# The modulation's matrix-vector product moved to TensorE, and another order of the first loads

## The chip, the cores and the metric

The kernel runs on one core of one Trainium2 chip. The metric is the device time of one execution in microseconds (us), the lower the better. Five engines run side by side, each with its own queue of instructions in program order: TensorE (PE in the profile, with its weight loads as PEld), VectorE (DVE), ScalarE (ACT), GpSimd (POOL), and SyncE, which here only issues the loads from memory (its queue is SPq in the profile).

## The reference, cut to what matters

Two transformer blocks run over 256 tokens (272 in the second block) of width 1024. The change touches the modulation of the first block only: one row vector, `silu(c)`, times a 1024 x 6144 matrix, whose 24 MB have to come from memory.

```python
def first_block(x, c, ada_w, ada_b, ln1_g, ln2_g, w_in, ...):
    cond = jax.nn.silu(c)                                   # [1, 1024]
    mod = (cond @ ada_w[l] + ada_b[l])[:, None, :]          # [1, 1, 6144]
    sh1, sc1, g1, sh2, sc2, g2 = jnp.split(mod, 6, axis=-1)
    h = rms_norm(x, ln1_g[l]) * (1.0 + sc1) + sh1
    x = x + g1 * hybrid_mixer(h, w_in[l], w_out[l], ...)    # two kinds of attention
    h = rms_norm(x, ln2_g[l]) * (1.0 + sc2) + sh2
    x = x + g2 * sparse_moe(h, router_w[l], ..., exp_w1[l], exp_w2[l], ...)   # 32 experts, top 4
    return x
# second_block(x, ...): attention, MLP, a linear recurrence, MLP
```

All is float32. `sc1` and `sh1` are needed ahead of the first product, `g1` by the products with `w_out`, `sc2` and `sh2` by the routing, `g2` behind the experts.

## The kernel before, in words

The kernel works in transposed form: a matrix of 256 tokens lies as eight tiles of [128 channels x 256 tokens]. In time it has three stretches: the first block up to the routing (0 to 262.9 us in the trace), the 32 experts (262.9 to about 1222 us), and the second block.

**Loads.** A list of 1 MB loads is written out by hand (`queue_pre`, L359) and issued in this order on SyncE by `Stream.pump` (L158), as soon as one of its buffers is free (`wraw` are four buffers, `wraw_r` three more at the start). One tile of the modulation's matrix is [128 x 2 x 1024]: two blocks of 128 rows, all 1024 columns of one of the six vectors. Four tiles q = 0 to 3 make a vector. In the names, s = 1 is `sc1`, 0 is `sh1`, 2 is `g1`, 4 is `sc2`, 3 is `sh2`, 5 is `g2`.

**Products.** A dense product takes a float32 weight apart into a high and a low part: ScalarE casts (L190), and GpSimd or VectorE subtracts (L192), as a string of letters, `st.cut`, says unit by unit. TensorE then runs three products per pair of tiles (L290 to L292). Its queue is in program order: a product that waits holds back all that is behind it.

**The modulation.** `ada(s, ...)` (L415) returns a list of steps. Eight steps `part(k)` each multiply a [128 x 1024] block with the column k of `cond` and add it to an accumulator, on VectorE (L435, L437), a few on ScalarE and GpSimd (L429, L431). Two steps `total(i)` transpose 4 x 128 columns each on TensorE (L449), sum them on VectorE (L452) and add them to the bias (L454). For s = 1 and 0 the steps run at the start, ahead of the first dense product; the last two blocks of s = 0 are taken in halves (L592). The steps of s = 2, 4, 3, 5 stand in the list `side`; `aux()` takes one between two dense products, if its load has been issued by then, and `side_to(n)` empties the list down to n steps. In the same way `fill()` takes one step of the attention from the list `bg`.

**Around it.** `mixer` runs the products with `w_in` (`dense_t`), interleaved with attention steps; `w_out_half(0)` and `w_out_half(4)` run the products with `w_out` and add them to the residual with `g1` (L949); between and behind them come the router's logits (L1032) and the routing (`route`), and then the experts' first products (L1440).

Of the kernel before, what the change touches and what calls it, by code (L numbers as in the profile page):

```python
# [8 lines left out]
F32 = mybir.dt.float32  # L9
# [4 lines left out]
AF = mybir.ActivationFunctionType  # L14
ALU = mybir.AluOpType
AX = mybir.AxisListType
# [4 lines left out]
S = 256  # L21
# [201 lines left out]
def add_cols(st, w, c0, ncol):  # L223

    for c in range(c0, c0 + ncol, 256):
        for k in range(0, w.shape[0], 1024):
            st.add([(_v("p (k n) -> p k n", k=8), w[k:k + 1024, c:c + 256].rearrange("(k p) n -> p k n", p=128))],
                   [lambda t, m=m: t.rearrange("p (k n) -> p k n", k=8)[:, :, m * 128:m * 128 + 128] for m in range(2)])
# [15 lines left out]
class Ker:  # L244
# [116 lines left out]
    def queue_pre(self):  # L361
# [3 lines left out]
        def add_ada(s, q):  # L365
            st.add([(_v("p (k n) -> p k n", k=2),
                     ada[q * 256:q * 256 + 256, s * 1024:s * 1024 + 1024].rearrange("(k p) n -> p k n", p=128))], ["raw"])
# [8 lines left out]
        for s in (1, 0):  # L376
            for q in range(4):
                add_ada(s, q)
        add_cols(st, w, 512, 256)
        cw = A["nsa_cmp_w1"][0]  # L380
# [34 lines left out]
    def ada(self, s, acc, pool, tag, first=0):  # L415

        nc = self.nc
        accs = [acc]

        def part(k):  # L420
            def go():
                if k % 2 == 0:
                    self.ada_t = self.st.get_raw()
                t, used = self.ada_t
                w = t[:, (k % 2) * 1024:(k % 2) * 1024 + 1024]
                if k in (1, 3, 5) and self.mid is not None:

                    b, t = self.mid[:, 0], self.mid[:, 1]
                    nc.scalar.activation(out=t if len(accs) > 1 else b, in_=w, func=AF.Copy, scale=self.cond[:, k:k + 1])  # L429
                    if len(accs) > 1:  # L430
                        nc.gpsimd.tensor_tensor(out=b, in0=b, in1=t, op=ALU.add)  # L431
                    else:
                        accs.append(b)
                elif k == first:
                    nc.vector.tensor_scalar(out=acc, in0=w, scalar1=self.cond[:, k:k + 1], scalar2=None, op0=ALU.mult)  # L435
                else:
                    nc.vector.scalar_tensor_tensor(out=acc, in0=w, scalar=self.cond[:, k:k + 1], in1=acc,  # L437
                                                   op0=ALU.mult, op1=ALU.add)
                if k % 2:
                    used()  # L440
            return go

        def total(i):
            def go():
                ps = pool.tile([128, 512], F32, name="adat", tag=tag)
                if len(accs) > 1:
                    nc.vector.tensor_tensor(out=acc, in0=acc, in1=accs.pop(), op=ALU.add)
                for m in range(4):
                    nc.tensor.transpose(ps[:, m * 128:m * 128 + 128], acc[:, i * 512 + m * 128:i * 512 + m * 128 + 128],  # L449
                                        self.c("ident"))  # L450
                t = self.pp.tile([128, 4], F32, name="adas", tag="adas", bufs=2)
                nc.vector.tensor_reduce(out=t, in_=ps.rearrange("p (m n) -> p m n", m=4), axis=AX.X, op=ALU.add)  # L452
                m4 = self.mod[:, 8 * s + 4 * i:8 * s + 4 * i + 4]
                nc.vector.tensor_tensor(out=m4, in0=t, in1=m4, op=ALU.add)  # L454
            return go

        return [part(k) for k in range(8)] + [total(i) for i in range(2)]
# [42 lines left out]
    def pre(self):  # L500
        nc, A, tc = self.nc, self.A, self.tc
        h = self.h
        X = slice(META, NT)
        ident = self.c("ident")
        with ExitStack() as ctx:
# [39 lines left out]
            self.mid = None  # L545
            acc2 = self.ar("s4", [128, 2, 1024], F32, "acc")
            acc = [acc2[:, i] for i in range(2)]
            s1, s0 = self.ada(1, acc[0], self.ps_d, "dps"), self.ada(0, acc[1], self.ps_d, "dps", 2)
            mid = [self.ar("s6", [128, 1024], F32, "mid"), vvt[:, 0:1024]]

            def by_scalar(k):

                def go():
                    if k == 0:
                        self.ada_t = self.st.get_raw()
                    t, used = self.ada_t
                    nc.scalar.activation(out=mid[k], in_=t[:, k * 1024:k * 1024 + 1024], func=AF.Copy, scale=self.cond[:, k:k + 1])
                    if k:
                        used()
                        nc.gpsimd.tensor_tensor(out=mid[0], in0=mid[0], in1=mid[1], op=ALU.add)  # L560
                return go

            s0 = [by_scalar(0), by_scalar(1)] + s0[2:]
            for f in s1[0:4]:
                f()
            rs = pp.tile([128, 3, S], F32, name="rs1", tag="hr")
            self.rsqrt(rs[:, 0], self.ss[:, :S], rs[:, 1], rs[:, 2], nc.gpsimd)
            xT = self.ar("s1", [128, 8, S], F32, "xs1")
            for k in range(8):
                nc.gpsimd.tensor_tensor(out=xT[:, k], in0=h[:, k, X], in1=rs[:, 0], op=ALU.mult)  # L570
            for f in s1[4:]:
                f()
            a1 = pp.tile([128, 8], F32, name="a1")
            nc.vector.scalar_tensor_tensor(out=a1, in0=self.mod[:, 8:16], scalar=1.0, in1=self.V8("ln1_g"),
                                           op0=ALU.add, op1=ALU.mult)
            for f in s0[0:2]:
                f()
            for k in range(8):
                nc.scalar.activation(out=xT[:, k], in_=xT[:, k], func=AF.Copy, scale=a1[:, k:k + 1])
            for f in s0[2:4]:  # L580
                f()
            nc.vector.tensor_tensor(out=acc[1], in0=acc[1], in1=mid[0], op=ALU.add)
            for f in s0[4:6]:
                f()
            nc.sync.dma_start(out=once, in_=A["once"])
            self.st.split_to(1)
            t, used = self.st.get_raw()
            for i in range(2):
                for k in (6, 7):
                    a = acc[1][:, i * 512:i * 512 + 512]  # L590
                    o = (k - 6) * 1024 + i * 512
                    nc.vector.scalar_tensor_tensor(out=a, in0=t[:, o:o + 512], scalar=self.cond[:, k:k + 1], in1=a,  # L592
                                                   op0=ALU.mult, op1=ALU.add)
            used()
            for f in s0[8:]:
                f()
# [8 lines left out]
            for s, a in ((2, 0), (4, 1), (3, 0), (5, 1)):  # L605
                self.side += [(k in (0, 2, 4, 6), f) for k, f in enumerate(self.ada(s, acc[a], self.ps_m, "m"))]

            self.side.insert(-2, (False, lambda: None))
# [10 lines left out]
    def mixer(self, H, L):  # L619
# [310 lines left out]
        self.mid = self.ar("s3", [128, 2, 1024], F32, "mid2")  # L930
        self.side_to(28)
# [23 lines left out]
        self.side_to(21)  # L955
# [4 lines left out]
        self.b1 = self.ar("b1", [64, 2048], F32R, "b1")  # L960
        self.route_early()
# [53 lines left out]
    def route_tile(self, m):  # L1015
# [35 lines left out]
        if m == 5:  # L1051
            self.side_to(11)
            self.route_bias()

    def route(self):
# [19 lines left out]

        self.h2h = self.ar("s3", [128, 2, 1024], F32R, "h2h")
# [87 lines left out]
        self.side_to(0)  # L1164
# [1075 lines left out]
```

## Time and profile before

| | us |
|---|---|
| median of 3 runs | 1898.0 (1895.3, 1898.0, 1903.77) |
| the profiled execution: its own time | 1897.58 |
| its span, from the first to the last instruction | 1895.5 |
| granted TensorE clock, mean share of full speed | 0.977 |
| PE busy | 1775.4 (94%) |
| DVE busy | 996.3 (53%) |
| ACT, POOL busy | 631.9 (33%), 403.4 (21%) |
| moved from memory | 549.60 MB, mean 290 GB/s |

The span and the time of the profiled execution differ by 2.1 us, which lie ahead of the first and behind the last instruction. The busy share is a mean over stretches that are limited by different things, so the table of stretches among the rows below is read first. In the timelines each row gives the start, the duration, the engine, the line of the kernel, the operation with its tile, and in square brackets how long the engine was idle before it and what ended that idle time. A float32 product leaves two records in the trace, one with the reduced type (fp32r) leaves one.

### The profile page before, as it was taken

Reading aid. Unit: us, or ns where it says so; the run is one execution under the profiler, and the core shown is the slowest. Engines: PE = TensorE matmul, PEld = TensorE weight load, DVE = VectorE, ACT = ScalarE, POOL = GpSimd, SP = SyncE. Lnnn points to the kernel's source line nnn. Section 1 sums busy time; section 2 is a strip of 40 time slices with the busy share of each in tenths; the row PEclk is TensorE's granted clock in tenths of the full one; section 3 lists DMA queues with packets and bytes.
Section 4 is the critical chain, followed back from the end, with each engine's and each line's share of the span. In section 5 each row is a group of like instructions: output and inputs, shape, how many; then the busy total and the mean of one; then the engine's idle time right before and its main releaser. Section 6 shows DMA issues by size and latency. Waiting matters only on the chain. (4 is left out here: it accounts for less than half of the span.)

```text
span 1895.5 us, 25891 instructions
## 1 busy us (share of the span) xinstructions
PE 1775.4 (94%) x10035; PEld 1107.9 (58%) x10035; DVE 996.3 (53%) x1620; ACT 631.9 (33%) x1110; POOL 403.4 (21%) x266
## 2 busy tenths in 40 slices
PE   3988779999999999999999999799999999889998
PEld 2866643333334343333434343387789999789986
DVE  7686744544444434444443444554575544986622
ACT  3444322111211101121110112255565544755633
POOL 4533310000000000000000000155333334554443
PEclk6999989999999999999999999899999999999999
DMA  9544789999999999999999999642245545345552
GB/s 340 207 150 134 252 326 376 423 425 424 423 425 423 425 424 406 424 423 425 423 426 423 400 424 423 225 163 74 65 134 178 179 165 169 112 133 174 182 187 80
DMA packets 183342, 549.60 MB, mean 290 GB/s; under 512 B 8656, under 2 KB 101968, under 8 KB 150256
## 3 DMA queue, kind: packets, MB, share of 16 engines
q1 hardware_dynamic: 182592, 545.99, 74.6%
q8 instruction: 80, 1.31, 0.3%
q0 software_dynamic: 432, 1.57, 0.3%
q14 instruction: 46, 0.38, 0.1%
q10 hardware_dynamic: 192, 0.35, 0.1%
HBM read 546.83 MB, written 1.05 MB: 289 GB/s over the span
## 5 line engine op out<-in xcount | busy, mean ns | idle before, releaser
L192 POOL TENSOR_TENSOR wsp<-wraw,wsp 128x1024 fp32r<-128x1024 f32 x134 | 329.6, 2463 | 1393.3 <-ACT wsp L190 1356.5
L290 PE MATMUL dps<-hn_hi,wsp 128*128 128x272 f32 (+1 forms) x832 | 248.1, 298 | 9.1 <-DVE h L1908 4.1
L190 ACT CAST wsp<-wraw 128x1024 fp32r<-128x1024 f32 x208 | 215.3, 1042 | 113.8 <-PE dps L292 51.1
L291 PE MATMUL dps<-hn_lo,wsp 128*128 128x272 f32 (+1 forms) x832 | 242.8, 292 | 1.9 <-DVE hn_lo L1636 1.9
L292 PE MATMUL dps<-hn_hi,wsp 128*128 128x272 f32 (+1 forms) x832 | 242.3, 291 | 0.0
L1571 DVE SCALAR_TENSOR_TENSOR h<-cb,vec,h 128x256 f32<-128x256 f32 x256 | 111.8, 479 | 225.4 <-PE cb L1567 225.4
L1440 PE MATMUL u<-wraw_s,xs 128*64 128x512 f32 x728 | 207.6, 602 | 0.9 <-DVE gl L1470 0.9
L1468 ACT COPY gl<-u 64x512 f32<-64x512 f32 x120 | 66.7, 582 | 417.9 <-PE u L1440 356.8
L1440 PE MATMUL u<-wraw,xs 128*64 128x512 f32 x648 | 195.2, 604 | 0.0
L290 PEld LDWEIGHTS dps<-hn_hi,wsp 128*128 128x128 f32 x832 | 161.0, 194 | 14.3 <-issue 5.8
L1440 PE MATMUL u<-wraw_r,xs 128*64 128x512 f32 x544 | 164.5, 608 | 0.0
L291 PEld LDWEIGHTS dps<-hn_lo,wsp 128*128 128x128 f32 x832 | 160.6, 193 | 3.9 <-DVE hn_lo L1636 3.0
L292 PEld LDWEIGHTS dps<-hn_hi,wsp 128*128 128x128 f32 x832 | 160.8, 193 | 0.0
L1470 DVE TENSOR_TENSOR gl<-u,gl 64x512 f32<-64x512 f32 x120 | 79.1, 680 | 140.8 <-ACT gl L1468 140.8
L192 DVE TENSOR_TENSOR wsp<-wraw,wsp 128x1024 fp32r<-128x1024 f32 x74 | 96.3, 1304 | 94.1 <-ACT wsp L190 93.9
L1440 PEld LDWEIGHTS u<-wraw_s,xs 128*64 128x64 f32 x728 | 54.7, 136 | 73.9 <-issue 65.6
L2004 DVE TENSOR_TENSOR y<-r 128x272 f32<-128x272 f32 (+1 forms) x64 | 52.9, 827 | 64.6 <-ACT r L2001 64.5
L1566 PE MATMUL cb<-st,y 128*128 128x256 f32 x256 | 80.1, 336 | 6.2 <-DVE h L1571 6.2
L1440 PEld LDWEIGHTS u<-wraw,xs 128*64 128x64 f32 x648 | 49.5, 136 | 61.4 <-issue 52.4
L1542 PE MATMUL y<-wraw_s,at 128*64 128x512 f32 x368 | 82.8, 594 | 0.0
L1566 PEld LDWEIGHTS cb<-st,y 128*128 128x128 f32 x256 | 48.4, 189 | 57.4 <-issue 41.3
L1542 PE MATMUL y<-wraw_r,at 128*64 128x512 f32 x336 | 77.3, 601 | 3.7 <-SPq L1246 3.7
(508 smaller groups left out, 3275.5 us busy)
## 6 DMA issues: line engine op xcount, KB each, us to landing
wraw_s<-in_exp_w SPq DMA_DIRECT2D x147, 1024.0 KB, 14.1
wraw_r<-in_exp_w SPq DMA_DIRECT2D x120, 1024.0 KB, 15.0
wraw<-in_exp_w SPq DMA_DIRECT2D x117, 1024.0 KB, 13.5
wraw<-in_mlp_w_up SPq DMA_DIRECT2D x32, 1024.0 KB, 5.4
wraw<-in_mlp_w_down SPq DMA_DIRECT2D x32, 1024.0 KB, 4.8
wraw<-in_ada_w SPq DMA_DIRECT2D x18, 1024.0 KB, 6.3
wraw<-in_sb_w_qkv SPq DMA_DIRECT2D x12, 1024.0 KB, 5.1
wraw<-in_lru_w_in SPq DMA_DIRECT2D x8, 1024.0 KB, 5.0
```

The costliest lines, as they stand in the source:

```text
L190: nc.scalar.copy(out=hv, in_=src)
L192: e.tensor_tensor(out=lv, in0=src, in1=lr, op=ALU.subtract)
L290: mm(o, lhsT=wh, rhs=xh, start=first, stop=False)
L291: mm(o, lhsT=wh, rhs=xl, start=False, stop=False)
L292: mm(o, lhsT=wl, rhs=xh, start=False, stop=last)
L1440: mm(u[n][64 * j:64 * j + 64], lhsT=xs[:, k, o:o + 64], rhs=w[:, ns], start=(q == 0), stop=(q == 3))
L1468: nc.scalar.copy(out=o, in_=u[n][64:128])
L1470: nc.vector.tensor_tensor(out=o, in0=u[n][R], in1=o, op=ALU.add)
L1542: mm(y[n][64 * j:64 * j + 64], lhsT=at[:, k, 0:64], rhs=w[:, ws], start=(q == 0), stop=(q == 3))
L1566: mm(o, lhsT=yh[:, m * 128:m * 128 + 128], rhs=st, start=True, stop=False)
L1571: nc.vector.scalar_tensor_tensor(out=h[:, m, META:NT], in0=o, scalar=self.mod[:, 40 + m:41 + m], in1=h[:, m, META:NT], op0=ALU.mult, op1=A ...
L2004: nc.vector.tensor_tensor(out=y[:, :n], in0=r[:, :n], in1=r[:, :n], op=ALU.mult)
```

## The change

`ada(s)` now has five steps. A step `part(q)` takes one whole tile: eight float32 products on TensorE (L436), two row blocks times four quarters of 256 columns. The weight is a column of `cond` broadcast to [128 x 32], so that quarter j is written to the partitions 32j to 32j+31 of one PSUM bank. Every one of the 32 partitions of a quarter holds the same sums. For s = 1 and 0 the four tiles add up in the bank (`whole`), and one VectorE copy (L442) brings [128 x 256] to SBUF; for the other vectors each tile is copied. The one step `total` selects one partition of each quarter by small products (L452), which also add up the four copies, and VectorE adds the bias (L455). The parts of s = 2, 4, 3, 5 use the PSUM bank "tp", which one in two of the attention's transposes also uses.

In the order of the loads the first tile of `w_in` moves from behind s = 0 to between s = 1 and s = 0, and the small table `once` moves ahead. The normalization's last steps and the products of x with it (before L570) go from GpSimd to VectorE, and the first two units of `w_in` are split ahead of the parts of s = 0, their low parts on VectorE. `side` has 20 entries where it had 41, and `side_to` gets other numbers.

```diff
--- before.py
+++ after.py
@@ -373,10 +373,11 @@
                 add_ada(*rest.pop(0))
 
         w = A["w_in"][0]
-        for s in (1, 0):
-            for q in range(4):
-                add_ada(s, q)
+        for q in range(4):
+            add_ada(1, q)
         add_cols(st, w, 512, 256)
+        for q in range(4):
+            add_ada(0, q)
...
-    def ada(self, s, acc, pool, tag, first=0):
+    def ada(self, s, whole=None):
+
 
         nc = self.nc
...
+        st, parts = {}, []
+
+        def bank(name):
+            pool, tag = whole or self.ada_bank
+            return pool.tile([128, 512], F32, name=name, tag=tag)
+
+        def part(q):
             def go():
...
+                t, used = self.st.get_raw()
+                if q == 0 or not whole:
+                    st["ps"] = bank("adap")
+                ps = st["ps"][:, 0:256]
+                for i in range(2):
+                    c = self.cond[:, 2 * q + i:2 * q + i + 1].to_broadcast([128, 32])
+                    for j in range(4):
+                        o = i * 1024 + j * 256
+                        nc.tensor.matmul(ps[32 * j:32 * j + 32], lhsT=c, rhs=t[:, o:o + 256],
+                                         start=(i == 0 and (q == 0 or not whole)), stop=(i == 1 and (q == 3 or not whole)))
+                used()
+                if whole and q < 3:
+                    return
+                x = self.acc[:, s % 2, q]
+                nc.vector.tensor_copy(out=x, in_=ps)
+                parts.append(x)
             return go
 
...
+        def total():
+            ps = bank("adat")
+
+            sel = self.c("ident").rearrange("p (j a) -> p j a", j=4)[:, :, 0]
+            for b in range(2):
+                for i, x in enumerate(parts):
+                    nc.tensor.matmul(ps[:, 4 * b:4 * b + 4], lhsT=x[:, b * 128:b * 128 + 128], rhs=sel, start=(i == 0),
+                                     stop=(i == len(parts) - 1))
+            m8 = self.mod[:, 8 * s:8 * s + 8].rearrange("p (j b) -> p b j", b=2)
+            nc.vector.tensor_tensor(out=m8, in0=ps[:, 0:8].rearrange("p (b j) -> p b j", b=2), in1=m8, op=ALU.add)
+
+        return [part(q) for q in range(4)] + [total]
 
...
+            self.acc = self.ar("s4", [128, 2, 4, 256], F32, "acc")
+            s1, s0 = self.ada(1, (pa, "tp")), self.ada(0, (self.ps_m, "ot"))
             rs = pp.tile([128, 3, S], F32, name="rs1", tag="hr")
-            self.rsqrt(rs[:, 0], self.ss[:, :S], rs[:, 1], rs[:, 2], nc.gpsimd)
+            self.rsqrt(rs[:, 0], self.ss[:, :S], rs[:, 1], rs[:, 2])
...
-                nc.gpsimd.tensor_tensor(out=xT[:, k], in0=h[:, k, X], in1=rs[:, 0], op=ALU.mult)
-            for f in s1[4:]:
+                nc.vector.tensor_tensor(out=xT[:, k], in0=h[:, k, X], in1=rs[:, 0], op=ALU.mult)
+            for f in s1:
                 f()
+            nc.sync.dma_start(out=once, in_=A["once"])
             a1 = pp.tile([128, 8], F32, name="a1")
             nc.vector.scalar_tensor_tensor(out=a1, in0=self.mod[:, 8:16], scalar=1.0, in1=self.V8("ln1_g"),
                                            op0=ALU.add, op1=ALU.mult)
...
             for k in range(8):
                 nc.scalar.activation(out=xT[:, k], in_=xT[:, k], func=AF.Copy, scale=a1[:, k:k + 1])
...
+            self.st.cut = "D"
+            self.st.split_to(2)
+            self.st.cut = "PPD"
+            for f in s0:
                 f()
...
             self.side = []
-            for s, a in ((2, 0), (4, 1), (3, 0), (5, 1)):
-                self.side += [(k in (0, 2, 4, 6), f) for k, f in enumerate(self.ada(s, acc[a], self.ps_m, "m"))]
-
-            self.side.insert(-2, (False, lambda: None))
+            self.ada_bank = pa, "tp"
+            for s in (2, 4, 3, 5):
+                self.side += [(k < 4, f) for k, f in enumerate(self.ada(s))]
...
-        self.side_to(28)
+        self.side_to(15)
...
-        self.side_to(21)
+        self.side_to(10)
 
...
+        self.ada_bank = self.ps_m, "m"
...
-            self.side_to(11)
+            self.side_to(5)
...
+        self.side_to(0)
...
-        self.side_to(0)
         self.st.limit = None
 
     def gates(self, pool):
```

The loads at the start, as SyncE issues them. Before, from the tile behind the first three of s = 1 on; `ada_w` is the modulation, `in_w_in` with 128x8x256 is the first dense weight:

```order
L170 DMA wraw<-in_ada_w 128x2x1024 x4
L170 DMA wraw_r_149<-in_ada_w 128x2x1024
L170 DMA wraw_r_153<-in_w_in 128x8x256
L170 DMA wraw_r_174<-in_w_in 128x8x128 x2
L170 DMA wraw<-in_nsa_cmp_w 64x16x128 x2
L170 DMA wraw<-in_w_in 128x8x128 x2
L170 DMA wraw<-in_nsa_cmp_w 64x16x128 x2
L170 DMA wraw<-in_w_in 128x8x128 x2
L585 DMA once<-in_once 128x1465
L170 DMA wraw_r_233<-in_ada_w 128x2x1024
```

And now, from the same place on:

```order
L170 DMA wraw<-in_ada_w 128x2x1024
L170 DMA wraw<-in_w_in 128x8x256
L170 DMA wraw<-in_ada_w 128x2x1024 x2
L170 DMA wraw_r_172<-in_ada_w 128x2x1024
L170 DMA wraw_r_182<-in_ada_w 128x2x1024
L170 DMA wraw_r_192<-in_w_in 128x8x128 x2
L170 DMA wraw<-in_nsa_cmp_w 64x16x128 x2
L554 DMA once<-in_once 128x1465
L170 DMA wraw<-in_w_in 128x8x128 x2
L170 DMA wraw<-in_nsa_cmp_w 64x16x128 x2
L170 DMA wraw<-in_w_in 128x8x128 x2
L170 DMA wraw_r_262<-in_ada_w 128x2x1024
```

The dense weight went ahead of the four tiles of s = 0, and `once` ahead of the second set of the compression's weights.

TensorE at the start, before: the sum of squares (L315), the two vectors' transposes, and the first dense products (`dps`):

```order
L315 MATMUL ss<-sq,cst 128x256 x8
L449 MATMUL adat<-cst,acc 128x128 x16
L290 MATMUL dps<-hh,wsp 128x256
L291 MATMUL dps<-hl,wsp 128x256
L292 MATMUL dps<-hh,wsp 128x256
```

And now, with eight parts in the place of sixteen transposes:

```order
L315 MATMUL ss<-sq,cst 128x256 x8
L436 MATMUL adap<-wraw_r_95,cond 32x256 x8
L436 MATMUL adap<-wraw_r_97,cond 32x256 x8
L436 MATMUL adap<-wraw_r_99,cond 32x256 x8
L436 MATMUL adap<-wraw,cond 32x256 x8
L452 MATMUL adat<-cst,acc 128x4 x2
L436 MATMUL adap<-wraw,cond 32x256 x16
L436 MATMUL adap<-wraw_r_172,cond 32x256 x8
L436 MATMUL adap<-wraw_r_182,cond 32x256 x8
L452 MATMUL adat<-cst,acc 128x4 x2
L290 MATMUL dps<-hh,wsp 128x256
```

In front of the first dense product TensorE now has 64 products L436, which wait for loads, where it had waited for VectorE's sums.

VectorE in `w_out_half(0)`, before, from the last attention steps on; the rows L949 add a finished product to the residual, the rows `acc` belong to s = 3:

```order
L437 SCALAR_TENSOR_TENSOR acc<-wraw,cond,acc 128x1024
L949 SCALAR_TENSOR_TENSOR h<-dps,vec,h 128x256
L286 TENSOR_TENSOR ol<-ot,oh 128x256
L437 SCALAR_TENSOR_TENSOR acc<-wraw,cond,acc 128x1024
L949 SCALAR_TENSOR_TENSOR h<-dps,vec,h 128x256
L447 TENSOR_TENSOR acc<-acc,mid_1658 128x1024
L452 TENSOR_REDUCE adas<-adat 128x4
L454 TENSOR_TENSOR vec<-adas,vec 128x4
L949 SCALAR_TENSOR_TENSOR h<-dps,vec,h 128x256
L452 TENSOR_REDUCE adas<-adat 128x4
L454 TENSOR_TENSOR vec<-adas,vec 128x4
```

And now the same place, with two copies of s = 5:

```order
L442 COPY acc<-adap 128x256
L915 SCALAR_TENSOR_TENSOR h<-dps,vec,h 128x256
L286 TENSOR_TENSOR ol<-ot,oh 128x256
L835 COPY ap<-tp 128x384
L915 SCALAR_TENSOR_TENSOR h<-dps,vec,h 128x256
L286 TENSOR_TENSOR ol<-ot,oh 128x256
L915 SCALAR_TENSOR_TENSOR h<-dps,vec,h 128x256 x2
L442 COPY acc<-adap 128x256
L915 SCALAR_TENSOR_TENSOR h<-dps,vec,h 128x256
L455 TENSOR_TENSOR vec<-adat,vec 128x2x4
L915 SCALAR_TENSOR_TENSOR h<-dps,vec,h 128x256
```

Two multiply-adds, a sum over `mid`, the reductions and the bias sums of s = 3 are gone from between the residual adds; two copies of [128 x 256] and one bias sum stand there.

## Rows read from the trace of the kernel before

**Rows 1.** The table of stretches: us, busy us of each engine (records), clock, DMA

```profile
14.40:30.40 16.00, 1.97 (x8) 1.57 (x8) 14.55 (x13) 6.38 (x12) 14.15 (x13) 0.56 1.04 410
...
100.00:158.60 58.60, 51.52 (x371) 37.33 (x369) 47.42 (x109) 28.88 (x98) 18.46 (x8) 1.00 0.45 141
158.60:190.00 31.40, 26.87 (x174) 19.52 (x172) 19.33 (x37) 10.68 (x30) 14.38 (x13) 1.00 0.40 105
...
210.00:224.00 14.00, 7.52 (x50) 7.20 (x50) 11.19 (x14) 4.38 (x4) 8.24 (x5) 0.88 0.95 323
224.00:250.00 26.00, 20.07 (x151) 18.65 (x150) 19.74 (x25) 4.10 (x9) 6.91 (x2) 0.93 0.93 368
250.00:262.90 12.90, 5.64 (x30) 4.30 (x28) 8.08 (x34) 6.65 (x17) 3.55 (x6) 0.57 0.78 326
...
300.00:1222.00 922.00, 911.03 (x4143) 357.83 (x4139) 408.93 (x706) 154.63 (x215) 0.00 (x0) 1.00 1.00 414
```

**Rows 2.** Waits of TensorE, 263 to 1222 us: total us, times, longest us

```profile
PE u L1442 <- DMA wraw<-in_exp_w: 0.9, 1, 0.9
```

**Rows 3.** Timeline of the start, to the first dense product

```profile
30.44 1.05 ACT L190 CAST wsp<-wraw_r 128x1024 fp32r<-128x1024 f32 x1 [0.57 <-DMA wraw_r<-in_w_in]
...
38.62 1.09 PE L449 MATMUL adat<-cst,acc 128*128 128x128 f32 x4 [14.84 <-DVE acc L592]
...
41.38 0.58 PE L290 MATMUL dps<-hh,wsp 128*128 128x256 f32 x1 [0.22 <-ACT hh L601]
```

**Rows 4.** Timeline of TensorE, first dense products: the last slow and first fast ones

```profile
46.75 0.41 PE L292 MATMUL dps<-hh,wsp 128*128 128x256 f32 x1
46.97 0.34 PE L290 MATMUL dps<-hh,wsp 128*128 128x256 f32 x1
...
47.38 0.28 PE L290 MATMUL dps<-hh,wsp 128*128 128x256 f32 x1
47.50 0.28 PE L291 MATMUL dps<-hl,wsp 128*128 128x256 f32 x1
```

**Rows 5.** DMA issues of 45.9 to 46.5 us: count, KB, us to landing

```profile
wraw_r<-in_ada_w SPq DMA_DIRECT2D x1, 1024.0 KB, 7.2
```

**Rows 6.** Timeline of TensorE: a product of 32 columns (L727) among others

```profile
61.09 0.94 PE L660 MATMUL hid<-once,wraw 128*128 128x31 f32 x7
...
62.19 0.28 PE L292 MATMUL dps<-hh,wsp 128*128 128x256 f32 x1
62.40 0.62 PE L727 MATMUL hs<-sq,once 128*32 128x256 f32 x2
62.95 0.39 PE L290 MATMUL dps<-hh,wsp 128*128 128x256 f32 x1
```

**Rows 7.** Timeline of TensorE in the experts: tiles of 64 columns

```profile
613.54 0.59 PE L1440 MATMUL u<-wraw_s,xs 128*64 128x512 f32 x1
613.55 0.59 PE L1440 MATMUL u<-wraw_r,xs 128*64 128x512 f32 x1
613.98 0.59 PE L1440 MATMUL u<-wraw_s,xs 128*64 128x512 f32 x1
```

**Rows 8.** Timeline of TensorE: the four transposes of a total

```profile
99.42 0.60 PE L449 MATMUL adat<-cst,acc 128*128 128x128 f32 x4
```

**Rows 9.** Waits of TensorE, 100 to 190 us

```profile
PE sc L830 <- ACT ap L848: 4.7, 4, 1.8
```

**Rows 10.** Waits of TensorE, 190 to 250 us

```profile
PE adat L449 <- DVE acc L447: 4.8, 1, 4.8
PE lt L1032 <- DVE h L949: 4.7, 4, 2.6
```

**Rows 11.** Timeline of VectorE and GpSimd behind the last total

```profile
238.08 4.53 POOL L1046 TENSOR_TENSOR b<-b1a,b 32x2048 fp32r<-32x2048 f32 x1 [11.70 <-ACT b L1045]
238.14 4.49 DVE L454 TENSOR_TENSOR vec<-adas,vec 128x4 f32<-128x4 f32 x1
```

**Rows 12.** VectorE by line, 41.4 to 250 us: busy us, mean ns, idle before

```profile
L437 DVE SCALAR_TENSOR_TENSOR acc<-wraw,cond,acc 128x1024 f32<-128x1024 f32 x20 | 31.0, 1548 | 0.0
```

More of the change, by code (lines that the diff above doesn't have):

```diff
@@ L413, in queue_pre @@
         more(len(rest))
-    def ada(self, s, acc, pool, tag, first=0):
+    def ada(self, s, whole=None):
         nc = self.nc
-        accs = [acc]
-        def part(k):
-            def go():
[L422 to L440, printed above, removed]
-            return go
[L443 to L457, printed above, removed]
@@ L544, in pre @@
                 self.square_in(k, h[:, k, X], S)
[L545 to L565, printed above, removed]
+            self.acc = self.ar("s4", [128, 2, 4, 256], F32, "acc")
+            s1, s0 = self.ada(1, (pa, "tp")), self.ada(0, (self.ps_m, "ot"))
             rs = pp.tile([128, 3, S], F32, name="rs1", tag="hr")
-            self.rsqrt(rs[:, 0], self.ss[:, :S], rs[:, 1], rs[:, 2], nc.gpsimd)
+            self.rsqrt(rs[:, 0], self.ss[:, :S], rs[:, 1], rs[:, 2])
             xT = self.ar("s1", [128, 8, S], F32, "xs1")
             for k in range(8):
-                nc.gpsimd.tensor_tensor(out=xT[:, k], in0=h[:, k, X], in1=rs[:, 0], op=ALU.mult)
-            for f in s1[4:]:
+                nc.vector.tensor_tensor(out=xT[:, k], in0=h[:, k, X], in1=rs[:, 0], op=ALU.mult)
+            for f in s1:
                 f()
+            nc.sync.dma_start(out=once, in_=A["once"])
             a1 = pp.tile([128, 8], F32, name="a1")
@@ L575, in pre @@
                                            op0=ALU.add, op1=ALU.mult)
-            for f in s0[0:2]:
-                f()
             for k in range(8):
                 nc.scalar.activation(out=xT[:, k], in_=xT[:, k], func=AF.Copy, scale=a1[:, k:k + 1])
[L580 to L595, printed above, removed]
+            self.st.cut = "D"
+            self.st.split_to(2)
+            self.st.cut = "PPD"
+            for f in s0:
                 f()
@@ L929, in mixer @@
             self.fill()
-        self.mid = self.ar("s3", [128, 2, 1024], F32, "mid2")
-        self.side_to(28)
+        self.side_to(15)
         g1 = self.mod[:, 16:24]
```

## The prediction

> **What bounds the kernel now.** I read the table of stretches first, because the busy share over the whole span (PE 94%) hides three different programs. In the experts, 300 to 1222 us, TensorE is busy for 911.0 of 922 us [rows 1], and among its waits there only 0.9 us stand behind a load [rows 2]. So the experts last as long as TensorE needs, and when the routing ends x us earlier the kernel ends x us earlier. The memory is full there too (414 GB/s, share 1.00), but its loads wait for TensorE to free buffers. The second block is untouched. What the change is worth is therefore the shift of the routing's end, at 262.9 us, and nothing else.
>
> In front of that the reader is to see a queue that is full with holes. At the start TensorE does 1.97 us of work in 16 [rows 1]: it waits for VectorE's multiply-adds, and its first transposes come at 38.62 us, with 14.84 us idle ahead of them; the first dense product starts at 41.38 [rows 3]. In 100 to 158.6 us TensorE is idle for 7.1 us, in 158.6 to 190 for 4.5, in 210 to 224 for 6.5, in 224 to 250 for 5.9, in 250 to 262.9 for 7.3 (stretch less busy time) [rows 1]. VectorE is 81% busy in the first of these (47.42 of 58.6), and 31.0 us of VectorE's work between 41.4 and 250 us are 20 multiply-adds of the modulation, 1.55 us each [rows 12].
>
> **The start.** The load of the first dense weight is the ninth megabyte before, and ScalarE, idle for it, begins its cast at 30.44 [rows 3]; so nine megabytes are in by 30.4 us. Now the ninth is the last tile of `sh1`. The memory gives 410 GB/s in this stretch [rows 1], a megabyte in 2.5 us, so the eight parts come at the pace of the loads, and seven are done when the last lands. TensorE's queue holds them behind the sum of squares, so two buffers come free some 3 us later than before; the loads ahead fill the queue until then, so I count nothing. Behind the last landing: one part (1.2 us at full clock, 2.3 at half; 1.8 taken), and then copy, selection, bias, and the first half of x. Before, the same tail from the first transposes to the first product took 41.38 - 38.62 = 2.8 us [rows 3], with longer pieces; I take 2.3. First product at 34.5, that is **-6.9** (-8.3 to -4.4: 33.1 with everything fast, 37 if buffers or the copy's queue delay it). The dense weight, its split and the moved work on VectorE lie beside this: they land ten microseconds before they are needed.
>
> The clock: TensorE's granted share is 0.56 in 14.4 to 30.4 us [rows 1], with almost nothing on it, and the first products step by 0.22 us until 46.97 and by 0.12 at 47.38, the lower (1.2 GHz) and the upper (2.4 GHz) level [rows 4]. From 41.38 to 46.97 that is 26 products and some 2.5 us lost. With parts on TensorE every 2.5 us it may be at full speed from the start; in 250 to 262.9 us, with 5.6 us of work spread over 12.9, the share was 0.57 all the same [rows 1], so it need not be. I take half, **-1.2** (-2.5 to 0).
>
> The first tile of `g1` is issued in 45.9 to 46.5 us and needs 7.2 [rows 5]: there at 53.1 to 53.7. Its part stands some 1.5 us ahead of the products L660 at 61.09 [rows 6], an estimate from the order of the queue; 8.1 us earlier that is 51.5. TensorE waits in order where VectorE waited before: **+1.7** (0 to +4.4).
>
> **Sixteen parts among the dense products.** Each has 8 float32 products of 256 columns on 32 columns of the array, 16 records. The row of that shape is L727: from 62.40 to 62.95 for its two records; 0.12 of these 0.55 us, and 0.09 ahead of it (0.21 for a step of 0.12 [rows 4]), and 0.11 behind (0.39 against 0.28), are the change of shape, 0.32 in all, which leaves 0.21 a record [rows 6]. Whether four quarters run beside each other no row shows. Two halves do: L1440's products of two tiles start at 613.54 and 613.55, the next at 613.98, 0.43 us for a pair with 512 columns [rows 7], 0.21 for 256. So a part costs 4 x 0.213 + 0.32 = 1.17 us with four at a time, 2.0 with two, 3.7 one by one. I take the first, since the halves overlap without loss: 16 x 1.17 = **+18.7**. All of it is on the path as far as TensorE is full.
>
> The Trainium skill ("TensorE: Matmul & The Clock Gate", Measured speedup vs the span model) has three column tiles of 32 at 2.38 times one, which is 0.79 of ideal each. By that, an estimate, a part is 3.41/(4 x 0.79) + 0.32 = 1.40 us and the forecast 3.7 us later, 1899. The pairs in [rows 7] show no such loss; no run here shows four.
>
> The four totals: 16 records with 128-column weights, at 0.11 each (7 from 61.09 to 61.87, within 0.94 [rows 6]), 1.8 us, in place of two times some 0.45 (the transposes of [rows 8], of which 0.36 is their own time to the next row and 0.08 the next row's). 4 x 0.9 = **+3.6** (0 to +5).
>
> **What VectorE gives back.** 31.0 us and the sums go from it; 16 copies of [128 x 256] come, shorter than a multiply-add. In 100 to 190 us, 11.6 us of TensorE's idle time, of which 4.7 are the score products that wait for ScalarE's exponentials [rows 9]. I take two thirds, **-8** (-11.6 to 0: nothing, if that chain is bound by its own length or if the copies delay it as the sums did). In 210 to 224 us the idle is 6.5, of which 4.8 is one wait of the transposes for VectorE's sum over `mid` [rows 10], which is gone: **-5.5** (-6.5 to -4.8 plus what a copy there costs). In 224 to 250 it is 5.9, of which 4.7 are the logits waiting for the residual [rows 10]; the sums ahead of it go, but 4.5 us are a bias sum that ran beside GpSimd's [32 x 2048] sum, both as long as each other [rows 11]. What VectorE then does beside that sum will be slow instead, so **-4** (-5 to -0.5). All parts end by then, which shortens the routing's cold stretch by perhaps **-1**.
>
> **The sum.** -6.9 - 1.2 + 1.7 + 18.7 + 3.6 - 8 - 5.5 - 4 - 1 = -2.6. The profiled execution took 1897.6 us, so 1895.0; the median of the runs is 0.4 above it. Within 0.5% (9.5 us) a measurement of this kernel can't tell a change.
>
> **Rivals.** (A) *VectorE's relief is nearly whole, and parts fall into holes.* For it: 24 us of idle time between 100 and 250, nearly all behind VectorE or ScalarE. Against: several of these waits are the attention's own chain. With all 11.6, 6.5 and 5.9 gone (-6.5 more), the full clock (-1.3) and the fast start (-1.4) it is 1886, with a few parts in the routing's holes 1885: faster.
>
> (B) *Only two quarters run at a time*, as all rows show. A part is 2.0 us: 16 x 0.85 = 13.6 more, 0.8 more at the start, 1909: slower. It decides from 1.9 us a part.
>
> (C) *They run one by one*, so that the change doesn't do what it says. Then 16 x 2.56 = 41 more; at the start eight parts of 3.7 from 14.4 us end at 44, the first product at 46.5 (+12), while the wait for `g1` goes (-1.7): 1946.
>
> (D) *The bank.* Each of the 16 parts waits for its bank, and the attention's transposes behind it wait for the copy in VectorE's queue. The nearest row is the score products' longest wait, 1.8 us [rows 9]. At 0.9 us a part it is 14 us, 1909, and from there slower; at 1.8, 1924. Against it: VectorE has 25 us less to do.
>
> **Chances.** The forecast 0.57 (its own range 1886 to 1904), A 0.24, B 0.08, D 0.07, C 0.04. Of the forecast's cases about 0.03 are under 1888.5 and none above 1907.5, so faster by over 0.5%: 0.27, within: 0.54, slower: 0.19 (B, C, D). The range 1882 to 1910 leaves out C, half of D and a little of A.
>
> **What would show it.** In the changed profile: the first dense product at 33 to 37 us, and the clock in the 20 us ahead of it; the records of four L436 starting within 0.05 us of each other and a part of 1.0 to 1.4 us among dense products (B: 1.9 to 2.1; C: 3.4 or more); waits of TensorE for the copy L442 under 4 us in sum (D: over 14); the waits for L447 and L949 gone or under 2 us; and the experts as long as before within 2 us. I am wrong if the routing ends where the start's gain alone puts it, or if the experts don't follow the routing's end.

## The result and the profile after

The changed kernel took 1916.1 us (median of 6) against 1897.3 us before (6 runs): 1.009 times as long, 95% interval 1.0066 to 1.0115. One of the six runs took 2927.0 us at a mean granted clock of 0.554 and is left out of the ratio. The kernel is slower, and outside the range that was given. The profiled execution of the changed kernel, the fastest of the six, took 1911.3 us, 13.7 us more than that of before, its span 1909.5 us.

The start and the parts came out as predicted. The rows that answer to [rows 3] and [rows 6], from the timeline of TensorE (start and duration in us, engine, line, operation, tile, records, idle time before):

```profile
31.31 1.94 PE L436 MATMUL adap<-wraw_r,cond 128*32 128x256 f32 x16 [0.57 <-DMA wraw_r<-in_ada_w]
33.80 1.01 PE L452 MATMUL adat<-cst,acc 128*128 128x4 f32 x4 [0.55 <-DVE acc L442]
35.67 0.58 PE L290 MATMUL dps<-hh,wsp 128*128 128x256 f32 x1 [0.86 <-ACT hh L569]
...
71.28 0.28 PE L292 MATMUL dps<-hh,wsp 128*128 128x256 f32 x1
71.49 1.07 PE L436 MATMUL adap<-wraw_r,cond 128*32 128x256 f32 x16
72.49 0.39 PE L290 MATMUL dps<-hh,wsp 128*128 128x256 f32 x1
```

The first dense product starts at 35.67 us, 5.7 earlier. A part among dense products holds 1.00 us until the next product starts: 16 records of 0.213 us one by one would be 3.4, so the four quarters do run beside each other (in the trace the four records of a row block's quarters start within 0.02 us, and the next four 0.22 us later).

What went wrong is in the table of stretches. The columns are the stretch and its length in us, the busy us (records) of PE, PEld, DVE, ACT and POOL, the granted clock, the share of the DMA engines, and GB/s:

```profile
36.00:42.00 6.00, 6.00 (x28) 5.81 (x28) 5.69 (x13) 4.55 (x10) 1.37 (x1) 0.50 1.11 297
42.00:49.00 7.00, 3.65 (x30) 3.44 (x30) 1.14 (x1) 3.39 (x6) 3.43 (x2) 0.99 1.16 254
49.00:66.00 17.00, 17.00 (x90) 15.67 (x88) 3.63 (x12) 5.18 (x12) 4.80 (x5) 0.50 0.98 346
66.00:80.00 14.00, 14.00 (x121) 11.03 (x120) 4.06 (x13) 4.66 (x11) 2.26 (x3) 1.00 0.57 174
182.00:209.50 27.50, 27.50 (x95) 19.43 (x95) 4.95 (x12) 3.91 (x11) 4.70 (x2) 0.50 0.12 39
```

In two stretches, 17.0 and 27.5 us long, TensorE is busy all the time and its clock is at the lower of its two levels (1.2 GHz, 0.50). Two more, at 90 and 124 us, last 3.5 us each. Before, the clock was at 1.00 from 47 to 190 us:

```profile
47.00:190.00 143.00, 130.22 (x920) 101.40 (x919) 101.89 (x203) 63.59 (x178) 58.76 (x33) 1.00 0.51 164
```

At the upper level the work of these four stretches would have taken about half as long. That is an estimate of 25.8 us lost, half of 17.0 + 27.5 + 7.0.

To see where the time goes I set the 240 groups of dense products (three products each, counted in order of time) against each other. The table gives by how many us the group of a number starts later than in the profiled execution of before (its lag; negative: earlier). Later sections use the other columns.

```
group   before   changed  mixer only  start only  sum+hold   hold40
          us     kernel   (e4)        (e2)        (f2)       (h1)
   0     41.4     -5.7      0.2        -5.4        -5.7      -5.8
  16     50.6     -2.5      0.2        -3.0        -2.8      -1.8
  24     57.0      2.3      0.2         2.5        -2.7      -1.9
  32     64.2      6.4      1.3         8.5        -1.6      -0.7
  64     83.1     14.2      7.6        10.9         3.4       4.3
 112    123.9     20.5     13.0        10.8         8.2       9.0
 144    158.8     16.6      9.0        10.8         4.2       5.0
 176    190.1     28.4     20.8        10.7         2.5       3.4
 200    218.9     22.2     14.7        10.8        -3.7      -2.8
 239    248.0     19.9     12.7        11.4        -7.0      -7.9
```

The changed kernel loses at 0.5 of the clock between groups 16 and 32 (8.9 us; f2, at 1.00 there, loses 1.2), and between 144 and 176 (11.8 us; f2 gains 1.7). The experts' first product comes at 282.6 us, 19.7 later than the 262.9 of before.

Each long stretch stands behind a wait of TensorE. The rows of the first, of TensorE and ScalarE:

```profile
44.40 0.28 PE L292 MATMUL dps<-hh,wsp 128*128 128x256 f32 x1
48.03 0.38 PE L290 MATMUL dps<-hh,wsp 128*128 128x256 f32 x1 [3.35 <-ACT vvt L612]
...
45.55 1.04 ACT L190 CAST wsp<-wraw 128x1024 fp32r<-128x1024 f32 x1 [5.00 <-DMA wraw<-in_w_in]
46.50 1.47 ACT L612 COPY vvt<-dps 64x240 f32<-64x240 f32 x4
```

TensorE is now ahead of the memory. ScalarE, in program order, stands at the cast of a weight that lands at 45.5 us; the copies that empty TensorE's bank are queued behind it. The second, of TensorE, VectorE and GpSimd (`hb` are products that use 32 rows of the array):

```profile
178.18 0.28 PE L494 MATMUL dps<-wsp,hh 128*128 128x256 f32 x1
180.66 0.69 PE L708 MATMUL hb<-hr,spread 32*128 32x256 f32 x2 [2.20 <-DVE ap L835]
...
177.67 2.46 DVE L305 TENSOR_TENSOR hr<-hr 32x256 f32<-32x256 f32 x1
180.06 0.54 DVE L835 COPY ap<-tp 128x384 f32<-128x384 f32 x1
...
177.44 2.41 POOL L192 TENSOR_TENSOR wsp<-wraw,wsp 128x1024 fp32r<-128x1024 f32 x1 [1.54 <-ACT wsp L190]
```

A product of VectorE on [32 x 256] takes 2.46 us and ends within 0.3 us of GpSimd's subtraction beside it; the same operation two lines above (L303) took 0.41. It is the kind of stretch that [rows 11] show. In the kernel before no subtraction ran beside L305, and it took 0.48 us. That the subtraction is the cause was not tried by itself.

Not all of the 19.7 us reach the end. The span is only 14.0 us longer, because the experts, from their first product to their last combining product, take 962.1 us for 966.1. Near their end TensorE waits at the branch for tokens over the limit, L1246 before and L1213 now (total us, times, longest us):

```profile
PE y L1542 <- SPq L1246: 3.7, 1, 3.7
...
PE y L1509 <- PEq L1213: 1.2, 1, 1.2
...
PE cb L1533 <- DVEq L1213: 0.5, 1, 0.5
```

Behind the longer wait the clock of the kernel before is at 0.50 from 1207.6 to 1211.0 us. From the start of the experts' last product `u` of the first layer to the end of their last combining product `cb` it is 35.6 to 35.7 us in all four profiles with the four vectors on VectorE (before, e2, f4, g1) and 32.0 to 32.6 in all ten with them on TensorE. Why the branch waits less there was not tried.

### The profile page after: what moved, and what is told of

It reads as the page before. It is cut to its first block, busy times and chain, and to the rows that moved or that the text cites. A ratio compares the mean times of both kernels' runs of the same rounds, so it can differ in the third digit from the quotient of the medians.

```text
span 1909.5 us, 26638 instructions
## 1 busy us (share of the span) xinstructions
PE 1817.4 (95%) x10443; PEld 1133.3 (59%) x10443; DVE 921.9 (48%) x1588; ACT 624.0 (33%) x1103; POOL 365.9 (19%) x248
## 5 line engine op out<-in xcount | busy, mean ns | idle before, releaser
L192 POOL TENSOR_TENSOR wsp<-wraw,wsp 128x1024 fp32r<-128x1024 f32 x134 | 322.9, 2412 | 1429.3 <-ACT wsp L190 1396.1
L1407 PE MATMUL u<-wraw_s,xs 128*64 128x512 f32 x728 | 207.5, 602 | 0.9 <-DVE gl L1437 0.9
L1407 PE MATMUL u<-wraw_r,xs 128*64 128x512 f32 x648 | 195.2, 604 | 0.0
L1407 PE MATMUL u<-wraw,xs 128*64 128x512 f32 x544 | 164.2, 607 | 0.0
L1407 PEld LDWEIGHTS u<-wraw_r,xs 128*64 128x64 f32 x648 | 49.5, 136 | 61.5 <-issue 52.7
L1411 PEld LDWEIGHTS u<-b,P 64*64 64x64 f32 (+1 forms) x128 | 16.8, 132 | 103.5 <-issue 103.5
## 6 DMA issues: line engine op xcount, KB each, us to landing
wraw<-in_exp_w SPq DMA_DIRECT2D x120, 1024.0 KB, 14.9
wraw_r<-in_exp_w SPq DMA_DIRECT2D x117, 1024.0 KB, 13.7
```

Of the source, the lines that this page charges most:

```text
L192: e.tensor_tensor(out=lv, in0=src, in1=lr, op=ALU.subtract)
L1407: mm(u[n][64 * j:64 * j + 64], lhsT=xs[:, k, o:o + 64], rhs=w[:, ns], start=(q == 0), stop=(q == 3))
```

## The experiments

Two theories. **K**: the work is worth about what was forecast, and the clock makes the loss: two waits let it fall, and it stays low though TensorE is busy. **W**: the 16 parts and four totals are simply more than VectorE's relief gives back. Kernels that ran together share the runs of the kernel before; their medians (1897.5 to 1898.6) are left out below, and a ratio is to them.

**e1: more work, whose results nobody reads.** 34 products fill the two waits:

```diff
+        self.n_dt = getattr(self, "n_dt", 0) + 1
+        if self.n_dt == 2:
+            for _ in range(16):
+                self.nc.tensor.matmul(ps[:, 256:512], lhsT=wh[:, 7], rhs=xh(7), start=True, stop=True)
...
+                if group == 1 and i == 0:
+                    d = pa.tile([128, 512], F32, name="dmy", tag="tp")
+                    for _ in range(18):
+                        nc.tensor.matmul(d[:, 0:256], lhsT=H(0)[:, 0:128], rhs=H(0), start=True, stop=True)
```

> The changed kernel with 34 more products of 256 columns on TensorE whose results nobody reads: 16 behind the second dense tile, where it waits 3.35 us at 44.4 us, and 18 ahead of the first hb product at 178.5 us, where it waits 2.20 us. Theory K (the clock: the two waits let TensorE's clock fall, and 17 and 27 us of dense work then run at half speed, which costs 8.5 and 13.6 us): with less idle time the stretches at 0.5 are gone or much shorter, and the time is 1894 to 1905 us. Theory W (the added 16 parts and totals are simply more work than VectorE's relief gives back): the dummies cost 0 to 4 us more, 1916 to 1920 us.

Measured: 1904.1 us, ratio 1.0047 (1.0020 to 1.0074), 12 us less than the changed kernel, with more work. Its ten runs spread from 1898.5 to 1917.5 us, and the profile is of the fastest. The table of stretches:

```profile
49.00:66.00 17.00, 17.00 (x156) 15.07 (x156) 5.14 (x21) 6.75 (x16) 4.86 (x4) 1.00 1.07 382
66.00:174.50 108.50, 105.31 (x841) 77.89 (x841) 53.58 (x145) 45.46 (x130) 34.58 (x24) 1.00 0.55 170
175.00:195.50 20.50, 20.50 (x66) 13.81 (x66) 4.30 (x10) 2.38 (x6) 2.51 (x2) 0.51 0.15 52
```

In the same 17 us TensorE now runs 156 records in the place of 90, at 1.00. W falls. The second fall came all the same, and this time not behind a wait:

```profile
167.58 2.31 PE L714 MATMUL dmy<-hh 128*128 128x256 f32 x18
169.98 0.69 PE L716 MATMUL hb<-hr,spread 32*128 32x256 f32 x2
...
171.50 0.69 PE L716 MATMUL hb<-hr,spread 32*128 32x256 f32 x2
172.13 1.95 PE L452 MATMUL adat<-cst,acc 128*128 128x4 f32 x16
...
174.82 1.22 PE L716 MATMUL hb<-hr,spread 32*128 32x256 f32 x2
```

It stands behind a total, 16 records of 4 columns, and so do the two short falls of the changed kernel (totals at 87.1 and 121.6 us, falls at 90 and 124). But behind e1's own totals at 78.9 and 111.9 us the clock stays at 1.00.

**e2: the start alone**, the other four vectors on VectorE as before.

> The start as in the changed kernel (products on TensorE for sc1 and sh1, its order of loads); the other four vectors by VectorE as before. Theory K: the first dense product comes 5.7 us earlier, but the wait of 3.4 us at 44 us and the slow stretch behind it (8.5 us) stay, since they come from the order of the loads, and the fall at 182 us is gone: 1900 to 1906 us. Theory W: the start's gain is left and the added work is gone: 1890 to 1893 us.

Measured: 1907.5 us, 1.0072 (1.0046 to 1.0098). With none of the added parts in the mixer it is slower than before, against W, and 1.5 us above K's range. Its column above is the clearest of all: 3.0 us ahead at group 16, 10.9 behind at 64, and nearly constant from there on. Between lies one stretch:

```profile
47.50:78.00 30.50, 30.48 (x137) 28.89 (x137) 6.79 (x22) 8.71 (x18) 5.86 (x5) 0.50 0.73 247
```

**e3: the table `once` loaded later**, so that the awaited weight comes earlier: the line `nc.sync.dma_start(out=once, ...)` moves behind the parts of s = 0.

> The changed kernel with the load of the table once (0.73 MB) put back behind the second set of the compression's weights. Theory K: the weight that ScalarE waits for until 45.5 us lands 2 us earlier, TensorE's wait of 3.35 us falls under 1.5, the clock does not fall at 49 us, and 8 to 12 us come back: 1904 to 1908 us. If the clock falls all the same, the wait alone: 1913 to 1915. Theory W: 1913 to 1916 us.

Measured: 1905.8 us, 1.0047 (1.0018 to 1.0076), within K's range in the median. But its profile is of an execution of 1915.0 us in which the clock fell at 48 us all the same: the wait got shorter (2.40 us, where under 1.5 was expected), group 16 came 1.3 us earlier, and that was not enough there. Behind its long totals at 92.0 and 125.0 us the clock stays up. It does not settle what the order of `once` is worth.

**e4: the parts of s = 2, 4, 3, 5 alone**, start and loads as before.

> The start and the loads as in the kernel before, the parts of the other four vectors on TensorE as in the changed kernel. Theory K: no fall at 49 us; without one at 182 the added work (18 us of parts, 4 of totals) is met by VectorE's relief: 1897 to 1902; with one (other timing, so it may come at another place) 1908 to 1914 us. Theory W: the start's gain is lost and all of the added work stays: 1919 to 1923 us.

Measured: 1906.8 us, 1.0034 (1.0008 to 1.0060), far under W's range; the profiled execution, of 1908.9 us, lies in K's range with a fall. There is no fall at 49 us, none behind the long totals at 82.0 and 115.1, and one from 174 to 201.5 us, behind the same wait as in the changed kernel:

```profile
173.11 0.69 PE L784 MATMUL hb<-hr,spread 32*128 32x256 f32 x2 [2.20 <-DVE ap L911]
```

Its column prices the terms without the start: a part costs 1.1 us (the lag grows by 1.0 to 1.2 from part to part at full clock), and the lag reaches 13.0 us by group 112. It then falls by 4.0 by 144 although two parts lie there, grows by 11.8 by 176, where the clock falls, and falls by 8.1 by 239, in the products with `w_out`.

**f1, f2, f3: shorter totals, with both groups of unread products, and with the first group alone.** VectorE adds up the four parts of a vector, so that a total has 4 records:

```diff
-                x = self.acc[:, s % 2, q]
-                nc.vector.tensor_copy(out=x, in_=ps)
-                parts.append(x)
+                x = self.acc[:, s % 2, 0]
+                if parts:
+                    nc.vector.tensor_tensor(out=x, in0=ps, in1=x, op=ALU.add)
+                else:
+                    nc.vector.tensor_copy(out=x, in_=ps)
+                    parts.append(x)
```

> The changed kernel, but the four parts of s = 2, 4, 3, 5 are added up by VectorE (an add from PSUM in the place of a copy), so that a total has 2 products of 4 columns (4 records) in the place of 8 (16 records, 1.95 us). No products beside the work. Theory T (the totals' small products let the clock fall): the stretches at half speed behind the totals at 90 and 124 us are gone, those at 49 and 182 us, which stand behind waits of 3.4 and 2.2 us, stay; with 4 x 1.3 us less on TensorE 1905 to 1910 us. Theory V (only the waits do it): all four stretches stay, 1910 to 1912 us.

Measured: 1909.0 us. The falls behind the totals at 90 and 124 us are gone, the two behind waits stay (47 to 77.5 and 183.5 to 207.5 us): as T said. It does not show T, since e3 and e4 have no falls there either, with long totals.

> The same with both groups of products whose results nobody reads (16 behind the second dense tile, 18 ahead of the first hb product), which gave 1904 us with the long totals and left one slow stretch from 175 us on. Theory T: that stretch, which followed a total at 172 us, is gone, and with the shorter totals the time is 1886 to 1891 us, faster than both. Theory V' (the mixture of hb products and short dense groups lets it fall there): it stays, 1897 to 1900 us.

Measured: 1891.2 us, ratio 0.9981 (0.9956 to 1.0006): 18 us less than f1 by 34 unread products; no difference from the kernel before is shown. In its profile (an execution of 1886.5 us) the clock does not fall between 42 and 235.5 us:

```profile
42.00:235.50 193.50, 182.62 (x1485) 141.20 (x1483) 89.95 (x243) 76.43 (x209) 61.34 (x37) 1.00 0.61 199
```

> The same with the first group of 16 unread products only. If the wait of 2.2 us ahead of the first hb product is enough by itself, the clock falls there and 10 to 14 us are lost against the kernel with both groups: 1898 to 1903 us. If it takes wait and total together: as the kernel with both, 1886 to 1891 us.

Measured: 1896.4 us, under the range for a fall, and 5 us above f2 in the median. Both profiles run alike to group 144 (4.2 us of lag each). Then the 18 products decide: f2 has 2.5 us of lag at 176, f3 13.1, behind the same wait of 2.20 us that the changed kernel has:

```profile
168.30 1.07 PE L715 MATMUL hb<-hr,spread 32*128 32x256 f32 x2 [2.20 <-DVE ap L842]
...
168.50:192.50 24.00, 24.00 (x78) 16.44 (x77) 4.01 (x9) 2.73 (x4) 4.72 (x2) 0.50 0.14 45
```

So the wait alone is enough (f3), and with the wait filled the clock stays (f2). That a long total is enough is not shown: of the 13 that the profiles of the changed kernel, e1, e3 and e4 have at the upper level, 3 have a fall behind them.

All 14 profiles together bear the waits out. These are TensorE's waits of 1 us and more from 42 to 285 us that began at the upper level, and how many had a fall in them or within 4 us of their end:

| wait | number | with a fall |
|---|---|---|
| 1.0 to 1.9 us | 49 | 3 |
| 2.0 to 2.2 us | 9 | 8 |
| 2.4 to 4.8 us | 31 | 31 |

The one of 2.0 to 2.2 us without a fall is in g1 (2.08 us at 191.3). The kernel before has four waits of 2 us and more there, all from 188 us on.

**f4: the start alone with the first group of unread products.**

> The start on TensorE and its order of loads, the other four vectors on VectorE, and the 16 unread products behind the second dense tile. Without them this kernel took 1907.5 us, with a slow stretch from 47.5 to 78 us, and ran a constant 10.8 us behind the kernel before from there on. If that stretch alone made the loss, it is gone and the kernel stays 2 to 4 us ahead: 1893 to 1896 us. If the early start loses by its waits for loads, 1900 us or more.

Measured: 1897.1 us, 1.0013 (0.9976 to 1.0050), above the expectation, though 10 us below e2. In its profile (1901.7 us) the fall came later, at 57.5 us, and lasted 14 us. It stands behind a wait of 1.24 us at 54.2 us; what let it fall there was not tried.

**g1: the control**, the same 34 products in the kernel before.

> Control: the kernel before, with the same 34 products whose results nobody reads at the same two places (16 behind the second dense tile, 18 ahead of the first hb product). There TensorE does not wait at the first place and 0.82 us at the second, and its clock does not fall between 47 and 190 us. Theory K: there is nothing to win, 34 x 0.12 less the wait is 1 to 3.5 us lost: 1898 to 1902 us. If unread products gained by anything else than the clock (a better place for what follows, say), it would be faster than the kernel before by several us, as the changed kernel was.

Measured: 1899.3 us, 1.0002 (0.9982 to 1.0021). In the profile they cost 1.7 us at the first place and about 1 at the second. So unread products gain nothing in the median where there is no fall to prevent. Its ten runs lie within 1897.5 to 1901.5 us, where 8 of the 29 of before beside them lie at 1904.7 to 1907.1; what makes that upper group of the kernel before is not known.

**g2, g3, h1: towards a better kernel.** g2 adds a third group of 28 ahead of the router's bias product (L977), g3 has 24 products at either of the first two places, h1 is g2 with 40 at the first.

> The kernel with the summed parts and both groups of unread products (1891 us), and a third group of 28 ahead of the router's bias product, where TensorE waits 3.63 us at 236.8 us for VectorE and its profile shows half speed from 236 to 259.5 us, with 14.8 us of work in it. Theory K: if the clock then stays up, up to 7 us come back, if it falls at the next wait (4.6 us at 248.7) 3 to 4: 1884 to 1888 us in the median. Without effect of the clock: 1891 to 1893.

Measured: 1886.3 us, 0.9943 (0.9918 to 0.9969), within K's range. Part of the step from f2 is a matter of shares: five of f2's ten runs and five of g2's twelve lie in an upper group (above 1894), and either group moves by some 3 us.

> The kernel with the summed parts, with 24 unread products at either place in the place of 16 and 18. Its forerunner's runs fall into two groups, 1885 to 1888 and 1894 to 1902 us. If the second group are executions in which the remaining wait of 1.57 us at the first place still lets the clock fall, most runs are now at 1885 to 1889. If the groups have another cause, they stay as they are, 1 us later.

Measured: 1888.5 us, 0.9962 (0.9936 to 0.9988); six of ten runs lie at 1886.7 to 1889.2, the others above 1893: the groups stay. The profiles of g2 and g3 happened to be of the upper group, and show why: half speed from 50 to 77.5 and 80.5 us, behind waits of 2.93 and 2.60 us at the first place.

> The kernel with three groups of unread products (median 1886.3 us, seven runs at 1882 to 1888 and five at 1895 to 1900), with 40 unread products at the first place in the place of 16. The profile of its forerunner was one of the slow five: 2.93 us of TensorE's wait at 48.6 us were left, and half speed ran from 50 to 77.5 us. If that is what parts the two groups, 24 more products (2.9 us) cover the wait: the upper group is gone, all runs lie within 1883 to 1890 us, the median at 1885 to 1888. If the groups have another cause, four in ten runs stay above 1894.

Measured: 1886.4 us, 0.9926 (0.9903 to 0.9950), all six runs between 1882.9 and 1888.7. The upper group is gone (by chance, at g2's share, six runs would miss it in some 4 of 100 cases), and the clock is up from 42 to 235 us:

```profile
42.00:235.00 193.00, 185.98 (x1516) 145.04 (x1515) 88.38 (x243) 76.44 (x209) 59.89 (x37) 1.00 0.61 198
```

This version is faster than both kernels, 0.7% under the kernel before. About 3 us of its 12 are the shorter end of the experts (32.6 us for 35.7).

## Why the prediction was wrong, by its own steps

- **The clock** is the step that failed. The prediction had it as a term of the start alone, -1.2 us with -2.5 to 0 as its ends, and read the mixer's clock of 1.00 [rows 1] as given, which put its change there at nothing. By an estimate it was worth about +22 against before: 25.8 us in four stretches, less what before lost in its own two short falls behind 190 and 217 us (3.5 us each, half of that lost). With the forecast of -2.6 that makes 19.7, and the experts' first product came 19.7 us later; that the two agree to the tenth is luck. The sum also had waits, but priced each at its length: behind 3.35 and 2.20 us of waiting came a further 8.5 and 13.8 us (half of 17.0 and 27.5; the columns give 7.7 and 13.5 against f2). The Trainium skill ("TensorE: Matmul & The Clock Gate", Loop structure matters more than you think) warns that long waits for loads between products leave TensorE slow for the products that follow; I did not weigh it. The trace agrees about the fall, with 0.50 behind either wait, and the second was no wait for a load.
- **The start**: 35.67 us, -5.7 for a forecast of -6.9, in the range. The half speed of the first products stayed (36 to 42 us at 0.50), so the gain of clock taken there did not come. It was also no gain to keep: being early brought TensorE up against the loads, and the wait of 3.35 us, which the kernel before does not have, came from that.
- **The wait for the first tile of `g1`** (+1.7) did not come, since TensorE was late by then. The wait stood at a place that the prediction did not name, ScalarE's cast with the copies behind it.
- **The parts**: 1.1 us in e4 for 1.17; 16 x 1.1 = 17.6 for +18.7. Rivals B (2.0 us) and C (3.7 us) are wrong. By the loss per tile in the Trainium skill (same page, Measured speedup vs the span model) a part was an estimated 1.40 us; the trace shows 1.00 from its start to the next product, and the measurement decides.
- **The totals**: 1.95 us for 1.8. That the clock fell behind some of them was in no term.
- **VectorE's relief** was under-sized. In 100 to 190 us (-8) the profile of f2, without a fall, has its lag go from 5.4 (group 80) to 2.5 us (176) although seven parts and two short totals, some 8.9 us, lie there: 11.8 us given back, an estimate, of which some 1.8 are before's own transposes. In the products with `w_out` (-5.5 and -4) e4 gives 8.1 back although three parts and a total, some 5.3 us, lie in it: 13.4, again with some 1.8 us of transposes.
- **The routing's** -1 did not come: from the last dense group to the experts' first product it is 14.7 us, 14.9 before.
- **Rival D**, the bank: TensorE's waits for the copy L442 are 2.2 us at the transposes and 0.9 at a total, in sum 3.1, under the 4 that the prediction set for D to be wrong. The parts L436 themselves wait 1.8 us in all for ScalarE to empty their bank (L837):

```profile
PE tp L833 <- DVE acc L442: 2.2, 2, 1.4
PE hb L708 <- DVE ap L835: 2.2, 1, 2.2
PE adap L436 <- ACT ap L837: 1.8, 2, 1.4
...
PE adat L452 <- DVE acc L442: 0.9, 1, 0.9
```

- **The end follows the routing**: the experts themselves do, but their end does not. They end 4.0 us sooner behind their first product than before, where the prediction allowed 2, and with 1.7 us in the second block the 19.7 us become 14.0.

Without falls the sum up to the experts was about right, in part by luck. f2, at 1.00 from 42 to 235.5 us, is 7.0 us ahead at group 239 and 6.2 at the experts' first product (256.7 us); of this up to 4 x 1.3 = 5.2 us are its shorter totals, which leaves 1.0 to 1.8 for a forecast of 2.6 (its 34 unread products lie mostly in waits). But sizes that were off cancel in it: of the lead at the start some 3.6 us are lost by group 16, at a wait that was in no term, and VectorE gave back more than was forecast. So the parts, the totals and the start held, and the place where the kernel is most sensitive was missing.

## What to carry to other kernels

A wait of TensorE costs its length, and then what its clock costs behind it: look for every wait of about 2 us or more that a change makes (here the clock fell behind 39 of 40 such waits, and behind 3 of 49 shorter ones), also where it shifts TensorE against loads or puts VectorE beside GpSimd, and read the granted clock of the stretch behind. Where a wait can't be taken away, products that nobody reads can hold the clock: here 34 of them, some 4 us of work, were worth 18 us. Whether small sums with few columns let the clock fall is open; added up by VectorE they cost TensorE 1.3 us less each.

## What the runs showed that was not expected

- A low clock outlasts its cause. In the changed kernel it stayed at 0.50 for 17.0 and 27.5 us and in e2 for 30.5, with TensorE busy throughout; in f2 the same products, 49 to 66 us, ran at 1.00. In these stretches short products (31 columns, or 32 rows) stand between the dense ones; whether they keep it low was not tried.
- One fall seems to part the executions of one kernel into two groups. g2's runs lie at 1882 to 1888 and 1895 to 1900 us, and its one profile, of the upper group, shows the fall; with the wait covered (h1) six runs of six are in the lower group. A single profile can be of either.
- VectorE's [32 x 256] product L305 took 2.46 us beside GpSimd's subtraction, and 0.48 in the kernel before, where no subtraction ran beside it.
- The branch behind the experts costs TensorE less when the four vectors are on TensorE: their last stretch takes 32.1 us for 35.7, a gain that no term had.
